# Strassen's weight sums in a feed-forward stage: which engine adds them, and the order of seven products

## The chip, the cores and the metric

The kernel runs on one core of one Trainium2 chip. The metric is the device time of one execution in microseconds (us), as the median of several runs. A profiled execution gives, beside its own time, the span from the first to the last instruction and a trace of every engine: PE (TensorE), whose weight loads are listed apart as PEld, DVE (VectorE), ACT (ScalarE), POOL (GpSimd) and SP (SyncE, which only issues transfers here).

## What is computed

One decoder layer on 512 tokens of width 1024, all in float32: a norm, two mixers (Mamba-2 and gated DeltaNet), a merge and projection, and then the feed-forward part, which alone is touched:

```python
FFN_HIDDEN = -(-8 * D_MODEL // (3 * 256)) * 256      # 2816
h = rmsnorm(x, norm_ffn_w[l])                        # 512 x 1024
gate, up = jnp.split(h @ w_ffn_in[l], [FFN_HIDDEN], axis=-1)   # w_ffn_in: 1024 x 5632
x = x + (jax.nn.silu(gate) * up) @ w_ffn_down[l]
...
return rmsnorm(x, final_norm_w)
```

## The kernel before

Every float32 matrix product is made of three matmuls. `split` (L265) parts a tile into a high half (`whi`, a cast on ACT) and a rest (`wlo`, a subtraction on DVE); `three` (L342) issues high x high, high x low and low x high into one PSUM bank. A weight block of 512 x 256 (512 KB) is a unit of the `stream`: it is loaded by SP (`fetch`, L303), split, and multiplied.

The hidden width 2816 is cut into 11 blocks of 256 columns (`fp`, 0 to 10). Block 0 is done in the plain way. Blocks 1 to 10 are done by Strassen's scheme in Winograd's form: the gate columns and the up columns of a block, each in an upper and a lower half of 512 rows, are four weight blocks b11, b12, b21 and b22, and seven products P1 to P7 of 512 x 256 weights with 512 x 256 activations take the place of eight. Their weights are b11 (P1), b21 (P2), t1 = b11 + b12 (P5), t3 = b12 + b22 (P7), b22 (P3), t2 = t1 + b22 (P6) and t4 = b21 + t2 (P4); signs are taken up by the sums of activations, which `h2_sums` makes once. A product is 24 matmuls of 256 columns (2 x 4 x 3).

Before the change (`ffn_units`, L1272) three tiles are loaded a block: x = b11, y = b22 and z = b21. The sums are made in them by transfers that POOL issues and that add to their destination (`gp.dma_start(..., accum_op=ALU.add)`). Once x has been split for P1, b12 is added to it (t1); once t1 has been split, b22 is added (t2); then z, after its own split, receives x (t4). y receives b12 after its split (t3). So each sum waits until the tile's earlier value has been read, and t4 also for t2 to land.

`ffn_block` (L1382) runs the products in the order `ORDER` into the PSUM banks that `BANK` names: A to F, one tile `pw` each. P1 and P2 share bank A: ACT copies P1 out of it to `p1`, and P2 is then added on top of it. `ffn_post` (L1298) forms the four output blocks from the banks: silu of the gate halves on ACT, sums u2, u3, c22 and the two multiplications (`act`) on DVE.

PE, DVE and ACT run their instructions in the order in which the program issues them; a planner (`Weave`, L34) with its own clock decides when which thread issues. SP's and POOL's order is set by a scheduler at build time. `ahead(2, 3)` (L278), called half-way through a product, splits up to two units ahead of it and has loads issued up to three units ahead of the splits; `Source.post` runs what follows a split (here the adding transfers). Buffers: 3 `whi`, 3 `wlo`, 3 `wst` (pool `wp`), 5 of `m4` (L209, where x and y lie), 8 PSUM banks.

After block 10, `down_job` (L1412) multiplies by w_ffn_down (tiles `pdn`).

Of the kernel before, what the change touches and what calls it, by code (L numbers as in the profile page):

```python
# [10 lines left out]
AF = mybir.ActivationFunctionType  # L11
ALU = mybir.AluOpType
ENG = mybir.EngineType

P = 128
T = 512
NT = T // P
D = 1024
# [15 lines left out]
class Weave:  # L34
# [65 lines left out]
    def finish(self, *events):  # L100
        for e in events:
            self.done[e] = self.cur

    def until(self, *events):

        def left():
            return [e for e in events
                    if e not in self.done or self.done[e] + SLACK > self.clock["PE"]]
        while left():
            assert self.threads or all(e in self.done for e in events), left()  # L110
            self.clock["PE"] += 100.0
            self.tick()
# [64 lines left out]
def hybrid_block_kernel(  # L177
# [8 lines left out]
    x = x[0]  # L186
# [12 lines left out]
    def nm(s):  # L199
        uid[0] += 1  # L200
        return f"{s}_{uid[0]}"

    def psum(s="p"):
        return ps.tile([P, 512], F32, tag="p", name=nm(s))

    def b8(shape, dtype=F32, s="b8"):
        return ap.tile([P] + list(shape), dtype, tag="b8", name=nm(s), bufs=NB8)

    def m4(shape, dtype=F32, s="m4"):  # L209
        return ap.tile([P] + list(shape), dtype, tag="m4", name=nm(s), bufs=NM4)  # L210

    def s2(shape, s="s2"):
        return ap.tile([P] + list(shape), F32, tag="s2", name=nm(s), bufs=NS2)

    wv = Weave(nc)
    te, ve, ac, gp, sy = wv.te, wv.ve, wv.ac, wv.gp, wv.sy
    start, spawn, until, finish, tick, side = wv.start, wv.spawn, wv.until, wv.finish, wv.tick, wv.side
# [60 lines left out]
    def ahead(n_split, n_load):  # L278

        main = wv.cur  # L280
        for i in range(len(splits), min(at[0] + n_split, len(stream))):
            _, a, b = stream[i]
            while len(loads) <= i:
                load()
            wv.cur = max(wv.clock["PE"], loads[i][1])
            src = stream[i][0]
            if getattr(src, "keep", False):
                both = b8([2, a, b], F32R, "wkeep")
                hi, lo = both[:, 0], both[:, 1]
            else:  # L290
                hi = wp.tile([P, a, b], F32R, tag="whi", name=nm("whi"))
                lo = wp.tile([P, a, b], F32R, tag="wlo", name=nm("wlo"))
            split(hi, lo, loads[i][0])
            if callable(src):
                src.post()
            splits.append((hi, lo, wv.cur))
            if len(loads) < min(i + 1 + n_load, len(stream)):
                load()
        while len(loads) < min(len(splits) + n_load, len(stream)):
            load()  # L300
        wv.cur = main

    def fetch(src, a, b, pool=None):  # L303
        if pool:
            st = pool([a, b], s="wst")
        else:
            st = wp.tile([P, a, b], F32, tag="wst", name=nm("wst"))
        sy.dma_start(st, src)
        return st
# [21 lines left out]
    def unit():  # L331
        ahead(1, 0)
        hi, lo, ready = splits[at[0]]
        at[0] += 1
        wv.clock["PE"] = max(wv.clock["PE"], ready)
        return hi, lo
# [537 lines left out]
    for b in range(2):  # L874
        z = Batch()
# [386 lines left out]
    ffn.a = {}  # L1262
    ffn.act = []
    NB = FH // 256
    ORDER = ("P1", "P3", "P2", "P5", "P7", "P6", "P4")
    BANK = {"P1": "A", "P3": "F", "P2": "A", "P5": "D", "P7": "C", "P6": "B", "P4": "E"}

    def ffn_src(r, c, fp):
        off = (FH if c else 0) + 256 * fp
        return w_ffn_in[512 * r:512 * r + 512, off:off + 256].rearrange("(k p) c -> p k c", p=P)  # L1270

    def ffn_units(fp):  # L1272
        if fp == 0:
            return [(Source(lambda r=r, c=c: fetch(ffn_src(r, c, 0), 4, 256), keep=True), 4, 256)
                    for c in range(2) for r in range(2)]
        w = Batch()

        def get(name, r, c, pool=None):
            setattr(w, name, fetch(ffn_src(r, c, fp), 4, 256, pool))
            return getattr(w, name)  # L1280

        def add(dst, src):
            gp.dma_start(dst, src, accum_op=ALU.add)

        def t2_t4():
            add(w.x, ffn_src(1, 1, fp))
            add(w.z, w.x)

        return [(Source(g, p), 4, 256) for g, p in (
            (lambda: get("x", 0, 0, m4), lambda: add(w.x, ffn_src(0, 1, fp))),  # L1290
            (lambda: get("y", 1, 1, m4), lambda: add(w.y, ffn_src(0, 1, fp))),
            (lambda: get("z", 1, 0), None),
            (lambda: w.x, t2_t4),
            (lambda: w.y, None),
            (lambda: w.x, None),
            (lambda: w.z, None))]

    def ffn_post(fp):  # L1298

        v = ffn.act[fp]  # L1300
        lo, hi = slice(0, 256), slice(256, 512)

        def half(s_):
            t = s2([512], s_)
            return t, t.rearrange("p (j t) -> p j t", j=2)

        bk = ffn.banks[fp]

        def two(t):
            return t.rearrange("p (j t) -> p j t", j=2)  # L1310

        if fp == 0:
            for name, s_ in (("c11", lo), ("c21", hi)):
                yield [("P", fp, name)]
                ac.activation(v[:, :, s_], two(bk[name]), AF.Silu)
                yield [("P", fp, name[:2] + "2")]
                ve.tensor_tensor(v[:, :, s_], two(bk[name[:2] + "2"]), v[:, :, s_], ALU.mult)
            finish(("ffn", fp))
            yield True
            return  # L1320
        yield [("P", fp, "P1")]
        p1, _ = half("p1")
        ac.copy(p1, bk["A"])
        finish(("p1", fp))
        yield [("P", fp, "P2")]
        ac.activation(v[:, :, lo], two(bk["A"]), AF.Silu)
        yield [("P", fp, "P6")]
        u2, _ = half("u2")
        u3, _ = half("u3")
        ve.tensor_tensor(u2, bk["B"], p1, ALU.add)  # L1330
        ve.tensor_tensor(u3, bk["C"], u2, ALU.add)
        ve.tensor_tensor(u2, bk["F"], u2, ALU.subtract)
        ve.tensor_tensor(u2, bk["D"], u2, ALU.add)
        ve.tensor_tensor(v[:, :, lo], two(u2), v[:, :, lo], ALU.mult)
        c22, c22v = half("c22")
        ve.tensor_tensor(c22, bk["D"], u3, ALU.subtract)
        yield [("P", fp, "P4")]
        ve.tensor_tensor(u3, bk["E"], u3, ALU.add)
        yield HOP
        ac.activation(v[:, :, hi], two(u3), AF.Silu)  # L1340
        yield HOP
        ve.tensor_tensor(v[:, :, hi], c22v, v[:, :, hi], ALU.mult)
        finish(("ffn", fp))
        yield True
# [3 lines left out]
    def ffn_start(fp):  # L1348
        ffn.banks[fp] = {}
        if fp % 2 == 0:  # L1350
            ffn.pair = b8([2, 2, T], F32, "act")
        ffn.act.append(ffn.pair[:, fp % 2])
        spawn(ffn_post(fp))

    def product(p, a, w, first, last, each=None):

        for j in range(2):
            cs = slice(j * P, (j + 1) * P)
            for kk in range(4):
                three(p[:, 256 * j:256 * j + 256], (w[0][:, kk, cs], w[1][:, kk, cs]), (a[0][:, kk], a[1][:, kk]),  # L1360
                      first and j == 0 and kk == 0, last and j == 1 and kk == 3, skip_group_check=True)
                if kk % 2:
                    tick()
            if j == 0 and each:
                each()
# [16 lines left out]
    def ffn_block(fp):  # L1382
        ffn_start(fp)
        bk = ffn.banks[fp]
        for name in ORDER:
            until(("a", name), *([("p1", fp)] if name == "P2" else []))
            fresh = BANK[name] not in bk
            if fresh:
                bk[BANK[name]] = psum("pw")
            w = unit()  # L1390
            product(bk[BANK[name]], ffn.a[name], w, fresh, True, lambda: ahead(2, 3))
            finish(("P", fp, name))

    for fp in range(NB):
        job(lambda fp=fp: ffn_block(fp) if fp else ffn_first(), *ffn_units(fp))
# [3 lines left out]
    def act_split():  # L1399

        for fp in range(NB):
            yield [("ffn", fp), ("P", NB - 1, ORDER[max(0, (fp + 1) // 2 - 1)])]
            w = b8([2, 2, T], F32R, "actw")
# [117 lines left out]
```

## Time and profile before

| | |
|---|---|
| median of three runs (1053.76 to 1055.57) | 1055.55 us |
| the profiled execution | 1055.14 us |
| its span, first to last instruction | 1053.4 us |
| PE busy of the span | 1008.9 us (96%) |
| DVE, ACT, POOL busy | 58%, 43%, 11% |
| products of blocks 1 to 10 | 680.9 to 926.7 us of the span |
| mean granted TensorE clock, of full speed | 0.99 |

The profiled execution lies 1.74 us above its span and 0.04% under the median. A matmul's end is modelled, so that PE counts as busy while a matmul drains; how much PE could still do is read from the distance between the starts of matmuls rather than from its busy share. A wait is put down to what came last.

### The profile page before, as it was taken

How to read it: one execution, taken by the hardware profiler on the slowest of the kernel's cores; microseconds unless marked ns; L12 is line 12 of the kernel's file. 1: busy time of each engine (PE TensorE's matmuls, PEld its weight loads, DVE VectorE, ACT ScalarE, POOL GpSimd, SP SyncE). 2: the span in 40 equal slices, each digit the busy share in tenths (PEclk: the TensorE clock that was granted, in tenths of full speed). 3: DMA queues.
4: the chain of work that ended last, by engine and by line, in shares of the span. 5: the costliest groups of instructions: out<-in, count | busy, mean ns of one | idle time of the engine just before them, and what ended most of it. 6: DMA issues, size and time to landing. Idle time of an engine off the chain costs nothing. (4 is left out here: it accounts for less than half of the span.)

```text
span 1053.4 us, 15628 instructions
## 1 busy us (share of the span) xinstructions
PE 1008.9 (96%) x6394; PEld 890.8 (85%) x6394; DVE 611.3 (58%) x904; ACT 453.9 (43%) x831; POOL 118.0 (11%) x144
## 2 busy tenths in 40 slices
PE   7999999999999999999999999989888888899997
PEld 5888878888888888788998899988888878888886
DVE  5665899545566867832255544755555555682422
ACT  5466445467857472022344223633333333452322
POOL 2041012100101210000010000111211211100000
PEclk9999999999999999999999999999999999999999
DMA  6242332121124533233322521657777776542222
GB/s 189 77 166 60 87 95 80 42 81 41 41 61 145 175 100 100 79 104 98 93 88 80 191 90 60 161 123 154 144 148 153 160 150 131 101 133 90 98 80 81
DMA packets 96072, 114.03 MB, mean 108 GB/s; under 512 B 6218, under 2 KB 86247, under 8 KB 95232
## 3 DMA queue, kind: packets, MB, share of 16 engines
q1 hardware_dynamic: 78718, 92.06, 28.3%
q0 software_dynamic: 17280, 20.97, 12.7%
q8 instruction: 50, 0.82, 0.3%
q14 instruction: 22, 0.18, 0.1%
q10 hardware_dynamic: 2, 0.00, 0.0%
HBM read 105.63 MB, written 2.15 MB: 102 GB/s over the span
## 5 line engine op out<-in xcount | busy, mean ns | idle before, releaser
L153 DVE TENSOR_TENSOR wlo<-wst,whi 128x1024 fp32r<-128x1024 f32 x184 | 225.7, 1236 | 297.1 <-ACT whi L153 290.9
L153 ACT CAST whi<-wst 128x1024 fp32r<-128x1024 f32 x184 | 190.9, 1048 | 285.5 <-PE pw L164 101.0
L164 PE MATMUL pw<-h2w,whi 128*128 128x256 f32 x1120 | 209.1, 288 | 11.2 <-ACT whi L153 11.2
L164 PE MATMUL pw<-hhi,whi 128*128 128x512 f32 (+1 forms) x496 | 196.4, 396 | 1.6 <-ACT whi L153 1.6
L164 PE MATMUL pw<-hhi,wlo 128*128 128x512 f32 (+1 forms) x496 | 191.2, 385 | 2.3 <-DVE wlo L153 2.3
L164 PE MATMUL pw<-hlo,whi 128*128 128x512 f32 (+1 forms) x496 | 190.6, 384 | 0.0
L164 PEld LDWEIGHTS pw<-h2w,whi 128*128 128x128 f32 x1120 | 177.4, 195 | 14.9 <-ACT whi L153 14.9
L164 PE MATMUL pw<-h2w,wlo 128*128 128x256 f32 x560 | 163.3, 292 | 16.7 <-DVE wlo L153 16.7
L164 PEld LDWEIGHTS pw<-h2w,wlo 128*128 128x128 f32 x560 | 109.2, 195 | 22.5 <-DVE wlo L153 22.2
L164 PEld LDWEIGHTS pw<-hhi,wlo 128*128 128x128 f32 x496 | 93.6, 189 | 21.9 <-DVE wlo L153 3.0
L164 PEld LDWEIGHTS pw<-hhi,whi 128*128 128x128 f32 x496 | 93.8, 189 | 18.1 <-ACT whi L153 1.8
L164 PE MATMUL pdn<-whi,actw 128*128 128x512 f32 x352 | 108.8, 390 | 0.0
L164 PEld LDWEIGHTS pw<-hlo,whi 128*128 128x128 f32 x496 | 93.8, 189 | 16.3
L164 PEld LDWEIGHTS pdn<-whi,actw 128*128 128x128 f32 x352 | 66.3, 188 | 13.9
L164 PE MATMUL pdn<-wlo,actw 128*128 128x512 f32 x176 | 68.6, 390 | 0.0
L153 POOL DMA_DIRECT2D wst<-in_w_ffn_in_dram x30 | 38.9, 1295 | 158.5 <-DVE wlo L153 154.7
L153 DVE SCALAR_TENSOR_TENSOR acc<-pw,pg,acc 128x511 f32<-128x511 f32 (+2 forms) x72 | 53.6, 747 | 2.8 <-ACT acc L153 0.9
L164 PE MATMUL pw<-yg,whi 128*128 128x512 f32 x128 | 42.9, 416 | 0.0
L164 PEld LDWEIGHTS pdn<-wlo,actw 128*128 128x128 f32 x176 | 33.2, 188 | 6.7
L164 PE MATMUL pt<-whi,hhi 128*128 128x256 f32 x128 | 36.5, 285 | 0.0
L164 PE MATMUL pt<-wlo,mgh 128*128 128x256 f32 x128 | 36.3, 284 | 0.1
L164 PE MATMUL pt<-whi,mgh 128*128 128x256 f32 x128 | 36.4, 284 | 0.0
(264 smaller groups left out, 1511.0 us busy)
## 6 DMA issues: line engine op xcount, KB each, us to landing
wst<-in_w_in_dram SPq DMA_DIRECT2D x68, 512.0 KB, 3.8
wst<-in_w_ffn_in_dram SPq DMA_DIRECT2D x34, 512.0 KB, 3.5
wst<-in_w_ffn_in_dram POOLq DMA_DIRECT2D x30, 512.0 KB, 5.9
wst<-in_w_ffn_down_dram SPq DMA_DIRECT2D x22, 512.0 KB, 3.7
decay<-gcd SPq DMA_DIRECT2D x6, 1024.0 KB, 4.7
wst<-wst POOLq DMA_DIRECT2D x10, 512.0 KB, 4.6
wst<-in_w_proj_gdn_dram SPq DMA_DIRECT2D x8, 512.0 KB, 3.4
wst<-in_w_proj_ssm_dram SPq DMA_DIRECT2D x8, 512.0 KB, 3.4
```

Source lines behind the costliest of these rows:

```text
L153: return f(out_, *args, **kw)
L164: return self.eng.matmul(out_, lhsT, rhs, **kw)
```

## The change

It replaces how the weight sums are made, the order of the seven products and the way the outputs are summed.

- Loads: five a block (b11, b21, b22, and a tile each for t1 and t3) in place of three. t1's tile is loaded with b11 and t3's with b22, right away, not after a split.
- Transfers that add: two a block in place of four. Each adds b12, to t1's tile and to t3's, as soon as that tile has landed.
- DVE: two new additions of 128 x 1024 a block (`sums`): t2 = t1 + b22 into a tile of its own, and t4 = t2 + b21 in place. They follow t1's split.
- The tiles t1, t2 and t3 lie in `m4`; b11, b21 and b22 in `wst`.
- Products: P1, P2, P5, P6, P7, P3, P4 in place of P1, P3, P2, P5, P7, P6, P4. P4 goes into P7's bank C, so that five banks a block are used in place of six; it waits for c22, which reads P7.
- Output sums: u2, w, c22, w and u2, five in place of six, and two multiplications as before.

```diff
-    ORDER = ("P1", "P3", "P2", "P5", "P7", "P6", "P4")
-    BANK = {"P1": "A", "P3": "F", "P2": "A", "P5": "D", "P7": "C", "P6": "B", "P4": "E"}
+    ORDER = ("P1", "P2", "P5", "P6", "P7", "P3", "P4")
+    BANK = {"P1": "A", "P2": "A", "P5": "D", "P6": "B", "P7": "C", "P3": "F", "P4": "C"}
...
-        def add(dst, src):
-            gp.dma_start(dst, src, accum_op=ALU.add)
-
-        def t2_t4():
-            add(w.x, ffn_src(1, 1, fp))
-            add(w.z, w.x)
+        def add(dst, r, c):
+            gp.dma_start(dst, ffn_src(r, c, fp), accum_op=ALU.add)
+
+        def t1():
+            get("t1", 0, 0, m4)
+            add(w.t1, 0, 1)
+            return w.t1
+
+        def t2():
+            get("b22", 1, 1)
+            w.t2 = m4([4, 256], s="t2")
+            return w.t2
+
+        def t3():
+            get("t3", 1, 1, m4)
+            add(w.t3, 0, 1)
+            return w.t3
+
+        def sums():
+            ve.tensor_tensor(w.t2, w.t1, w.b22, ALU.add)
+            ve.tensor_tensor(w.b21, w.t2, w.b21, ALU.add)
 
         return [(Source(g, p), 4, 256) for g, p in (
-            (lambda: get("x", 0, 0, m4), lambda: add(w.x, ffn_src(0, 1, fp))),
-            (lambda: get("y", 1, 1, m4), lambda: add(w.y, ffn_src(0, 1, fp))),
-            (lambda: get("z", 1, 0), None),
-            (lambda: w.x, t2_t4),
-            (lambda: w.y, None),
-            (lambda: w.x, None),
-            (lambda: w.z, None))]
+            (lambda: get("b11", 0, 0), None),
+            (lambda: get("b21", 1, 0), None),
+            (t1, sums),
+            (t2, None),
+            (t3, None),
+            (lambda: w.b22, None),
+            (lambda: w.b21, None))]
...
         u2, _ = half("u2")
-        u3, _ = half("u3")
+        w, wv_ = half("w")
         ve.tensor_tensor(u2, bk["B"], p1, ALU.add)
-        ve.tensor_tensor(u3, bk["C"], u2, ALU.add)
-        ve.tensor_tensor(u2, bk["F"], u2, ALU.subtract)
-        ve.tensor_tensor(u2, bk["D"], u2, ALU.add)
-        ve.tensor_tensor(v[:, :, lo], two(u2), v[:, :, lo], ALU.mult)
+        ve.tensor_tensor(w, bk["D"], u2, ALU.subtract)
+        yield [("P", fp, "P7")]
         c22, c22v = half("c22")
-        ve.tensor_tensor(c22, bk["D"], u3, ALU.subtract)
+        ve.tensor_tensor(c22, w, bk["C"], ALU.subtract)
+        finish(("c22", fp))
+        yield [("P", fp, "P3")]
+        ve.tensor_tensor(w, bk["F"], w, ALU.add)
+        ve.tensor_tensor(v[:, :, lo], wv_, v[:, :, lo], ALU.mult)
         yield [("P", fp, "P4")]
-        ve.tensor_tensor(u3, bk["E"], u3, ALU.add)
+        ve.tensor_tensor(u2, bk["C"], u2, ALU.add)
...
-            until(("a", name), *([("p1", fp)] if name == "P2" else []))
+            until(("a", name), *{"P2": [("p1", fp)], "P4": [("c22", fp)]}.get(name, []))
```

**First place: PE at the end of P1.** In these rows `h2w` is a split activation, and a `pw` tile a PSUM bank. PE before, from the last matmuls of P1 (bank pw_926) to the first of what follows:

```order
L164 MATMUL pw_926_6585<-h2w_838_5801,whi_918_6529 128x256 x2
L164 MATMUL pw_926_6585<-h2w_838_5801,wlo_919_6530 128x256
L164 MATMUL pw_929_6614<-h2w_869_6119,whi_924_6568 128x256 [waits Activation_49]
L164 MATMUL pw_929_6614<-h2w_869_6119,whi_924_6568 128x256
L164 MATMUL pw_929_6614<-h2w_869_6119,wlo_925_6569 128x256 [waits DVE_49]
```

What follows P1 is P3, in another bank (pw_929). PE after the change, at the same place of a later block (bank pw_963):

```order
L164 MATMUL pw_963_6827<-h2w_838_5801,whi_955_6774 128x256 x2
L164 MATMUL pw_963_6827<-h2w_838_5801,wlo_956_6775 128x256
L164 MATMUL pw_963_6827<-h2w_839_5816,whi_959_6807 128x256 [waits Activation_49]
L164 MATMUL pw_963_6827<-h2w_839_5816,whi_959_6807 128x256
L164 MATMUL pw_963_6827<-h2w_839_5816,wlo_960_6808 128x256 [waits DVE_49]
```

Now P2 follows, in the bank that P1 has just filled, with a wait for ACT.

**Second place: the transfers of a block.** POOL before, where wst_935 is x, wst_939 is y and wst_943 is z of one block, and the next row belongs to the next block:

```order
L153 DMA wst_935_6666<-in_w_ffn_in_dram 128x4x256 [waits DMAHW6_49,DVE_49]
L153 DMA wst_939_6698<-in_w_ffn_in_dram 128x4x256 [waits DMAHW0_49,DMASW5_49,DVE_49]
L153 DMA wst_935_6666<-in_w_ffn_in_dram 128x4x256 [waits DMASW4_49,DVE_49]
L153 DMA wst_943_6729<-wst_935_6666 128x1024 [waits DMAHW7_49,DMASW7_49,DMASW6_49]
L153 DMA wst_963_6894<-in_w_ffn_in_dram 128x4x256 [waits DMAHW1_49,DVE_49]
```

Each of the four stands behind a transfer or a split of the same block. POOL after, two rows a block, t1 and then t3 (wst_923 and wst_932 of block 3, wst_952 and wst_961 of block 4, wst_982 of block 5):

```order
L153 DMA wst_923_6514<-in_w_ffn_in_dram 128x4x256 [waits DMAHW1_49,DMAHW0_49,DVE_49]
L153 DMA wst_932_6581<-in_w_ffn_in_dram 128x4x256 [waits DMAHW1_49,DMASW1_49,DVE_49]
L153 DMA wst_952_6744<-in_w_ffn_in_dram 128x4x256 [waits DMAHW5_49,DMASW0_49,DVE_49]
L153 DMA wst_961_6811<-in_w_ffn_in_dram 128x4x256 [waits DMAHW6_49,DMASW3_49,DVE_49]
L153 DMA wst_982_6975<-in_w_ffn_in_dram 128x4x256 [waits DMAHW2_49,DMASW2_49,DVE_49]
```

What is left waits for the tile's own load and for an earlier user of its buffer. SP after, where wst_917 and wst_928 are b21 and b22 of block 3; wst_942, wst_952, wst_961, wst_946 and wst_957 are b11, t1, t3, b21 and b22 of block 4; and wst_972 is b11 of block 5:

```order
L153 DMA wst_917_6479<-in_w_ffn_in_dram 128x4x256 [waits DMAHW6_49,DMAHW2_49,DVE_49]
L153 DMA wst_928_6548<-in_w_ffn_in_dram 128x4x256 [waits DMAHW3_49,DVE_49]
L153 DMA wst_942_6678<-in_w_ffn_in_dram 128x4x256 [waits DMAHW7_49,DMAHW4_49,DVE_49]
L153 DMA wst_952_6744<-in_w_ffn_in_dram 128x4x256 [waits DMAHW5_49,DMASW0_49]
L153 DMA wst_961_6811<-in_w_ffn_in_dram 128x4x256 [waits DMASW3_49]
L153 DMA wst_946_6709<-in_w_ffn_in_dram 128x4x256 [waits DMAHW3_49,DVE_49]
L153 DMA wst_957_6778<-in_w_ffn_in_dram 128x4x256 [waits DMAHW0_49,DVE_49]
L153 DMA wst_972_6909<-in_w_ffn_in_dram 128x4x256 [waits DMAHW4_49,DMAHW1_49,DVE_49]
```

The loads of t1 and t3 of block 4 stand ahead of its b21, right behind its b11, which takes the buffer of block 3's b11.

**Third place: DVE through one block.** Before, from the split of t1 (wst_935, which is read again as t2 two rows on) to the split of the next block's b11 and the output sums:

```order
L153 TENSOR_TENSOR wlo_960_6861<-wst_935_6666,whi_959_6860 128x1024 [waits DMASW4_49,PE_49,Activation_49]
L153 TENSOR_TENSOR wlo_962_6891<-wst_939_6698,whi_961_6890 128x1024 [waits DVE_49,DMASW5_49,PE_49,Activation_49]
L153 TENSOR_TENSOR wlo_966_6923<-wst_935_6666,whi_965_6922 128x1024 [waits DVE_49,DMASW6_49,PE_49,Activation_49]
L153 TENSOR_TENSOR wlo_970_6954<-wst_943_6729,whi_969_6953 128x1024 [waits DMASW7_49,PE_49,Activation_49]
L153 TENSOR_TENSOR wlo_974_6985<-wst_963_6894,whi_973_6984 128x1024 [waits DMAHW1_49,PE_49,Activation_49]
L153 TENSOR_TENSOR u2_976_7008<-pw_972_6971,p1_958_6850 128x512 [waits PE_49]
L153 TENSOR_TENSOR u3_977_7009<-pw_968_6940,u2_976_7008 128x512 [waits DVE_49]
```

The splits of t1, t3, t2 and t4 each wait for an adding transfer (DMASW). After, from the split of t1 to c22:

```order
L153 TENSOR_TENSOR wlo_965_6844<-wst_952_6744,whi_964_6843 128x1024 [waits DMASW6_49,Activation_49]
L153 TENSOR_TENSOR t2_958_6780<-wst_952_6744,wst_957_6778 128x1024 [waits DMAHW0_49]
L153 TENSOR_TENSOR wst_946_6709<-t2_958_6780,wst_946_6709 128x1024 [waits DVE_49]
L153 TENSOR_TENSOR wlo_968_6876<-t2_958_6780,whi_967_6875 128x1024 [waits PE_49,Activation_49]
L153 TENSOR_TENSOR wlo_971_6906<-wst_961_6811,whi_970_6905 128x1024 [waits DMASW7_49,PE_49,Activation_49]
L153 TENSOR_TENSOR wlo_975_6937<-wst_957_6778,whi_974_6936 128x1024 [waits PE_49,Activation_49]
L153 TENSOR_TENSOR u2_978_6961<-pw_973_6923,p1_966_6861 128x512 [waits PE_49]
L153 TENSOR_TENSOR w_979_6962<-pw_969_6891,u2_978_6961 128x512 [waits DVE_49]
L153 TENSOR_TENSOR wlo_981_6972<-wst_946_6709,whi_980_6971 128x1024 [waits Activation_49]
L153 TENSOR_TENSOR c22_984_6997<-w_979_6962,pw_977_6954 128x512 [waits DVE_49,PE_49]
```

Two additions (t2, and t4 into wst_946) now stand between the split of t1 and that of t2, only the splits of t1 and t3 wait for an adding transfer, and the output sums stand apart from each other.

## Rows read from the trace of the kernel before

**Rows 1.** The page, busy us (share of the span) and instructions of each engine.

```profile
PE 1008.9 (96%) x6394; PEld 890.8 (85%) x6394; DVE 611.3 (58%) x904; ACT 453.9 (43%) x831; POOL 118.0 (11%) x144
```

**Rows 2.** Windows, the stage's stretch: us, busy us of engines, clock, DMA share, GB/s.

```profile
681.00:926.60 245.60, 217.64 (x1682) 208.28 (x1681) 138.29 (x151) 94.11 (x108) 44.97 (x38) 0.98 0.70 140
```

**Rows 3.** Instructions of tile pw on PE: duration ns min/median/max, first and last start.

```profile
L164 PE MATMUL pw<-h2w,whi x1120: 274/283/415, 680.9 to 926.1; 128*128 128x256 f32 x187
```

**Rows 4.** PE's waits in 681 to 927: us in total, times, longest us.

```profile
PE pw L164 <- DVE wlo L153: 16.7, 26, 0.8
PE pw L164 <- ACT whi L153: 11.2, 16, 2.0
```

**Rows 5.** Timeline of PE: start us, us, instruction, [idle before <-releaser].

```profile
767.88 0.40 PE L164 MATMUL pw<-h2w,whi 128*128 128x256 f32 x2
768.12 0.28 PE L164 MATMUL pw<-h2w,wlo 128*128 128x256 f32 x1
768.71 0.50 PE L164 MATMUL pw<-h2w,whi 128*128 128x256 f32 x2 [0.31 <-ACT whi L153]
769.97 0.39 PE L164 MATMUL pw<-h2w,wlo 128*128 128x256 f32 x1 [0.76 <-DVE wlo L153]
...
773.74 0.50 PE L164 MATMUL pw<-h2w,whi 128*128 128x256 f32 x2 [0.88 <-ACT whi L153]
```

**Rows 6.** Chain of waits, pieces of one block and its last: start us, us, what.

```profile
757.11 0.69 POOL wst L153
...
761.74 1.25 POOL wst L153
...
767.82 4.72 DMA wst<-wst
...
772.64 1.05 ACT whi L153
...
781.61 0.83 POOL wst L153
...
926.69 115.93 PE pdn L164 x510
```

**Rows 7.** DMA, 706 to 902: queue packets, MB, share; issues with KB, us to landing.

```profile
q0 software_dynamic: 13744, 16.70, 54.4%
q1 hardware_dynamic: 10713, 11.52, 18.4%
...
wst<-in_w_ffn_in_dram POOLq DMA_DIRECT2D x24, 512.0 KB, 5.9
wst<-in_w_ffn_in_dram SPq DMA_DIRECT2D x19, 512.0 KB, 3.7
```

**Rows 8.** Timeline of all engines around the end of a P1.

```profile
755.98 0.28 PE L164 MATMUL pw<-h2w,wlo 128*128 128x256 f32 x1
756.10 0.40 PE L164 MATMUL pw<-h2w,whi 128*128 128x256 f32 x2
756.30 0.59 ACT L153 COPY p<-pw 128x512 f32<-128x512 f32 x1 [1.95 <-PE pw L164]
```

**Rows 9.** Groups of instructions, 706 to 926: count, busy us, mean ns, idle before.

```profile
L153 DVE TENSOR_TENSOR wlo<-wst,whi 128x1024 fp32r<-128x1024 f32 x63 | 75.6, 1222 | 88.9 <-ACT whi L153 88.9
L153 ACT CAST whi<-wst 128x1024 fp32r<-128x1024 f32 x63 | 64.3, 1044 | 110.5 <-DMA wst<-in_w_ffn_in_dram 53.9 <-DMA wst<-wst 29.5 <-PE pw L164 27.1
...
L153 DVE TENSOR_TENSOR u<-pw,u 128x512 f32<-128x512 f32 x33 | 22.7, 689 | 0.8
```

**Rows 10.** Timeline of DVE, a sum of two float32 tiles in SBUF.

```profile
673.97 1.22 DVE L153 TENSOR_TENSOR hq<-hq,hq 128x1024 f32<-128x1024 f32 x1
```

**Rows 11.** Windows of 1 us behind waits of block 1; the clock is third from the end.

```profile
701.00:702.00 1.00, 0.45 (x3) 0.45 (x4) 1.00 (x2) 1.00 (x2) 0.00 (x0) 0.93 1.07 366
702.00:703.00 1.00, 1.00 (x7) 1.00 (x7) 1.00 (x2) 0.14 (x1) 0.07 (x1) 0.50 0.30 88
...
705.00:706.00 1.00, 1.00 (x9) 1.00 (x9) 0.97 (x2) 0.14 (x1) 0.00 (x0) 0.86 0.83 109
```

More of the change, by code (lines that the diff above doesn't have):

```diff
@@ L1328, in ffn_post @@
         u2, _ = half("u2")
-        u3, _ = half("u3")
+        w, wv_ = half("w")
         ve.tensor_tensor(u2, bk["B"], p1, ALU.add)
-        ve.tensor_tensor(u3, bk["C"], u2, ALU.add)
-        ve.tensor_tensor(u2, bk["F"], u2, ALU.subtract)
-        ve.tensor_tensor(u2, bk["D"], u2, ALU.add)
-        ve.tensor_tensor(v[:, :, lo], two(u2), v[:, :, lo], ALU.mult)
+        ve.tensor_tensor(w, bk["D"], u2, ALU.subtract)
+        yield [("P", fp, "P7")]
         c22, c22v = half("c22")
-        ve.tensor_tensor(c22, bk["D"], u3, ALU.subtract)
+        ve.tensor_tensor(c22, w, bk["C"], ALU.subtract)
[3 more added lines that the diff above has]
+        ve.tensor_tensor(v[:, :, lo], wv_, v[:, :, lo], ALU.mult)
         yield [("P", fp, "P4")]
-        ve.tensor_tensor(u3, bk["E"], u3, ALU.add)
+        ve.tensor_tensor(u2, bk["C"], u2, ALU.add)
         yield HOP
-        ac.activation(v[:, :, hi], two(u3), AF.Silu)
+        ac.activation(v[:, :, hi], two(u2), AF.Silu)
         yield HOP
```

## The prediction, made before the changed kernel was run

> **What bounds the kernel now.** The page's busy shares come first: PE at 96% [rows 1], so at first sight nothing that feeds PE is worth anything. But a matmul's end is modelled, so I looked next at the stage that the change touches and at how far apart its matmuls start. The stage runs from the first matmul of block 1 at 680.9 us [rows 3] to the first `pdn` matmul at 926.7 [rows 6]: 245.8 us. It holds 10 blocks x 7 products x 24 = 1680 matmuls. Where PE waits for nothing, two of them take 0.24 us from start to start (767.88 to 768.12) [rows 5], so 0.12 us each, and 1680 x 0.12 = 201.6 us. **So 44.2 us of this stage, 4.4 us a block, are not PE's work**, though its windows row shows PE busy for 217.6 of 245.6 us [rows 2].
>
> Does that close? PE's waits there come to 16.7 + 11.2 = 27.9 us in 42 waits [rows 4]. Each also hides 0.16 us (a modelled duration of 0.28 less the distance of 0.12) and restarts 0.10 us slower (a pair of 0.50 behind a wait, 0.40 elsewhere) [rows 5]: 42 x 0.26 = 10.9. The mean clock of 0.98 takes 2% of 245.6 us, 4.9 [rows 2]. Together 43.7 of the 44.2: the loss is waits, and what the clock does after them.
>
> Whom PE waits for names the splits, on ACT and DVE, but both are far from busy there (94 and 138 of 246 us [rows 2]). The chain of waits shows what stands behind them. One block of it [rows 6]: POOL issues a transfer that adds at 757.11, the next (into t2) at 761.74, the last (t2 into t4) at 767.82, when t2 has landed; t4 has landed by 772.64, when ACT casts it, and PE starts on it at 773.74 [rows 5]; behind that come DVE's subtractions and output sums, and with the following split POOL is back at 781.61: 24.5 us later, one block. This loop through POOL, the transfers, ACT and DVE is longer than PE's 7 x 24 x 0.12 = 20.2 us, and sets the pace.
>
> **The change, part by part.** *The loop goes.* t1 and t3 are now loaded and added to without a split before them. In SP's order the loads of t1 and t3 of block n+1 stand right behind that of its b11, which needs only that b11 of block n has been split; that split is done while block n-1 runs its last products. A load takes 3.7 us, an adding transfer 5.9 [rows 7]; even with both of the latter in a row, 3.7 + 2 x 5.9 = 15.5 us, issued some 18 us into block n-1, they land some 12 us into block n of 21, and are wanted when block n+1 starts. I cost them at nothing under that cover; what they cost without it is the slower rival below. t2 and t4 need no transfer.
>
> *The load on the DMA engines* stays short of full. In 196 us, 16.70 MB (32 transfers of 0.524 MB) that add took 54.4%, so 3.33 us of all engines each, and 11.52 MB (22) of plain loads 18.4%, 1.64 each [rows 7]. A block asked for 4 x 3.33 + 3 x 1.64 = 18.2 us; now 2 x 3.33 + 5 x 1.64 = 14.9, of a block of some 21 us: 70%, hidden. b21 of block n+1 waits until P3's b22 is split, about 12 us into block n, and is split itself from 18 on; b22 waits for t4's split, about 15 us in, and is wanted by `sums` at 25: at 3.7 us each both are in time, by 2 and 6 us.
>
> *DVE* gains two sums of 128 x 1024 at 1.22 [rows 10] and loses one of 128 x 512 at 0.69 [rows 9]: 7 x 1.22 + 2 x 1.22 + 7 x 0.69 = 15.8 us a block in place of 14.1. That is 75% of 21 us, not a bound by its sum. Its order could still hurt: both sums stand ahead of t2's split. With P1 starting at 0, u2 runs to 0.9, silu on ACT to 1.6, the multiplication to 2.3, the split of t1 (cast 1.04 [rows 9] on ACT, then 1.22) to 3.9, the sums to 6.3, t2's split to 7.5; P6 starts at 9.6. About 2 us remain. Later splits and sums find their inputs some 2 to 3 us before they are due, and c22 has read bank C two us before P4 writes it. So hidden, zero.
>
> *P2 behind P1 in one bank* is the one wait that the change adds on PE's path. P2's first matmul may not touch the bank before ACT has copied it. P1's last matmul starts at 755.98 and ends at 756.26; ACT's copy starts at 756.30 and takes 0.59, to 756.89 [rows 8]; an ACT result lets PE go 0.05 later (a cast from 772.64 [rows 6] for 1.05, PE at 773.74 [rows 5]): 756.94. PE went on at 756.10 [rows 8], since P3 in another bank came next. So 0.84 us, and 0.10 for the restart: **0.94 us a block, 9.4 us in ten**. Nothing else on PE can fill it; queued behind are all the block's products. ACT is free when the copy is due, as the silu and the cast ahead of it end near 2.7 us and P1 at 2.9. In block 10 one cast of the activations (1.04) stands there too; I add 0.4, between 0 and 1.0. Below zero this term can't go: the bank is the same.
>
> *Block 1 and the stage's borders.* The activations of P6 and P7 are made in the old order, in time for their new places. t1 of block 1 is loaded and added to much earlier, behind loads of other stages, where before two loads of this stage stood: zero. P4 in P7's bank, one bank fewer: zero.
>
> *Sum.* 201.6 + 9.4 + 0.4 = 211.4 us in place of 245.8: 34.4 us less. The profiled execution was 1055.14 us, so **1020.7 us**; it stands 0.04% under the median of 1055.55, and I make nothing of that difference.
>
> **The rivals.**
>
> *A. The clock falls in every block.* Behind block 1's waits at 700 the granted clock is 0.93, then 0.50 for three us (703 and 704 read as 702), then 0.86 [rows 11]: half speed, 1.2 GHz, and 0.07 + 1.5 + 0.14 = 1.7 us lost. If the gap behind each P1 brought that, ten blocks lose 17 us: 1037.7. Against it: the stage's 4.9 us are about three such falls in ten blocks, though a block had four waits on average [rows 4], of 0.3 to 0.9 us and close together [rows 5]; one gap a block of 0.84 is less. The Trainium skill (TensorE: Matmul & The Clock Gate, section "A second HAM failure mode: psum-queue depth-cycling") speaks for A: short idles between groups of matmuls, with PSUM banks in rotation, make the clock go up and down. By that rule, the result is A's 1037.7; the trace so far bears it out in the minority of blocks. 8%.
>
> *B. DVE's queue comes late.* The sums leave about 2 us ahead of P6. If the load of b22 or a stretched instruction uses that up, each block loses another 0.5 to 1.5 us: 1025.7 to 1035.7. For it: DVE at 75%, strictly in order, and its output sums now wait for single products in between. Against it: every slack above is over 1 us. 18%.
>
> *C. Transfers still set the pace.* At 70% load a transfer may take longer than its median; if b21 or t1 is late in many blocks, half of the gain is lost: 1055.14 - 17.2 = 1037.9. 4%.
>
> *D. No cost behind P1.* If the copy were over before P2 is due, PE runs at 0.12 us throughout: 1055.14 - 44.2 = 1010.9. Rows 8 speak against it. 4%.
>
> *E. Slower: t1 lands late, and holds P2 up.* On ACT the cast of t1 stands ahead of the copy of P1, so that a late t1 delays the very next product. Say its load is held back by one block more than I read from SP's order, because its buffer or b11's comes free late: issued 18 us into block n, it lands at 21.7, the addition at 27.6, the cast ends at 28.7, the copy at 29.3; P2 was due at 21.1 + 2.9 = 24.0. Then a block takes 20.16 + 5.3 + 0.1 = 25.6 us in place of 24.6, so 1055.1 + 10 = 1065. It decides from 4.4 us of wait a block. The order after the change speaks against it: block 4's t1 stands ahead of block 4's b21. 3%.
>
> **How the numbers follow.** My forecast has 63%, A 8, B 18, C 4, D 4, E 3. The likeliest is the forecast, 1020.7. Its own bounds are 1019 (the cost behind P1 at its bare 0.84, nothing in block 10) to 1024 (some 0.3 us a block left). To hold 8 in 10 the range goes from 1016 to 1036, which takes in B (63 + 18 = 81%) and a few us below the bound for what the clock gives back at the stage's end. Faster by over 0.2%, which is about what a measurement of this kernel can tell from no change, are all cases but E and a small part of C: 0.96; within 0.2% 0.01; slower 0.03.
>
> **What would show it.** In the profile after: the stage from the first matmul of block 1 to the first `pdn` takes 211 us; PE's waits there are about ten of 0.8 us, released by ACT's copy to `p` (right), where casts and subtractions released them before; DVE's share of the stage rises from 56% to about 75%, the DMA share stays near 0.70, the clock is 1.00. Wrong: PE waits for `whi` or `wlo` in most blocks (B, C), ACT waits for an adding transfer before the cast of t1 (E), a clock of 0.5 behind each P1 (A), or waits at P2 that are missing (D).

## The result, and the profile after

The changed kernel takes **1020.58 us** in the median of four runs (1019.94 to 1021.14), the kernel before beside it 1055.56 (1053.76 to 1056.59): a ratio of 0.967, with a 95% interval of 0.9653 to 0.9687. 35.0 us are gone. The profiled execution took 1021.12 us, its span is 1019.4.

First the page after, busy us (share of the span) and instructions of each engine, as [rows 1]:

```profile
PE 996.5 (98%) x6394; PEld 885.7 (87%) x6394; DVE 630.2 (62%) x914; ACT 455.3 (45%) x831; POOL 96.1 (9%) x124
```

By busy shares hardly anything has happened: PE from 96% to 98%. The stage tells more. Its matmuls, then PE's waits in 676 to 900 (total us, times, longest), then the stretch as a windows row (us, busy us of PE, PEld, DVE, ACT, POOL, clock, DMA share, GB/s):

```profile
L164 PE MATMUL pw<-h2w,whi x1120: 280/283/387, 681.4 to 892.3; 128*128 128x256 f32 x187
```

```profile
PE pw L164 <- ACT p L153: 7.0, 10, 0.9
```

```profile
681.00:892.00 211.00, 203.99 (x1681) 201.96 (x1680) 160.39 (x165) 96.31 (x109) 21.83 (x17) 1.00 0.67 163
```

Against [rows 3, 4, 2]: the first matmul of the stage starts at nearly the same time (681.4, before 680.9), the last 33.8 us sooner (892.3, before 926.1). Of 42 waits for casts and subtractions none is left; ten are there that were not, one a block, all for ACT's copy `p`. DVE went from 56% to 76% of the stretch, the DMA share from 0.70 to 0.67, the clock from 0.98 to 1.00.

The chain of waits says whom the stage now waits for. The end of one block and the next, and the last block (start us, us, what):

```profile
706.19 20.43 PE pw L164 x168
726.62 0.02 issue
726.64 0.59 ACT p L153
727.24 0.04 issue
...
853.83 17.56 PE pw L164 x144
...
873.71 0.94 ACT actw L153
874.65 0.49 ACT p L153
...
875.19 17.53 PE pw L164 x144
892.72 3.43 PE pdn L164 x15
```

POOL and the transfers, which stood in each block of the chain before [rows 6], are not in it: it is PE for 20.43 us, the copy, PE again. P2 of the one block starts at 706.19, that of the next at 727.24 + 0.04 = 727.28: a block takes 21.09 us in place of 24.5. In block 10 the cast of the activations (`actw`, 0.94) stands ahead of the copy, and P2 starts at 875.19, 21.36 us after block 9's (853.83).

The hand-over in PE's timeline (start us, us, instruction, [idle before <-releaser]), P1's last matmul and P2's first pair:

```profile
705.23 0.28 PE L164 MATMUL pw<-h2w,wlo 128*128 128x256 f32 x1
706.19 0.50 PE L164 MATMUL pw<-h2w,whi 128*128 128x256 f32 x2 [0.68 <-ACT p L153]
```

Start to start that is 0.96 us where 0.12 is usual, so 0.84 lost, and the pair takes 0.50 where 0.40 is usual.

And DVE in the same place of the next block, whose P1 ends at 726.6:

```profile
726.10 1.23 DVE L153 TENSOR_TENSOR wlo<-wst,whi 128x1024 fp32r<-128x1024 f32 x1 [0.25 <-ACT whi L153]
727.24 1.22 DVE L153 TENSOR_TENSOR t<-wst,wst 128x1024 f32<-128x1024 f32 x1
728.49 1.23 DVE L153 TENSOR_TENSOR wst<-t,wst 128x1024 f32<-128x1024 f32 x1
729.63 1.22 DVE L153 TENSOR_TENSOR wlo<-t,whi 128x1024 fp32r<-128x1024 f32 x1
```

The split of t1, the two new sums, the split of t2, without a gap. t2's rest is there at 730.85. P6 is due two products after P2's start, at 727.28 + 0.10 + 2 x 24 x 0.12 = 733.1: 2.3 us of slack.

Last the DMA from 706 to 892 (queue: packets, MB, share; issues with KB and median us to landing), as [rows 7]:

```profile
q1 hardware_dynamic: 20552, 21.61, 36.8%
q0 software_dynamic: 8448, 8.39, 29.9%
...
wst<-in_w_ffn_in_dram POOLq DMA_DIRECT2D x16, 512.0 KB, 7.0
```

Two adding transfers a block in place of four. Each takes longer to land than before, 7.0 us in place of 5.9, and nobody waits for it.

### The profile page after: what moved, and what is told of

The parts are those of the page before. It is cut to its first block, busy times and chain, and to the rows that moved or that the text cites. A ratio compares the mean times of both kernels' runs of the same rounds, so it can differ in the third digit from the quotient of the medians.

```text
span 1019.4 us, 15625 instructions
## 1 busy us (share of the span) xinstructions
PE 996.5 (98%) x6394; PEld 885.7 (87%) x6394; DVE 630.2 (62%) x914; ACT 455.3 (45%) x831; POOL 96.1 (9%) x124
## 5 line engine op out<-in xcount | busy, mean ns | idle before, releaser
L153 DVE TENSOR_TENSOR wlo<-wst,whi 128x1024 fp32r<-128x1024 f32 x174 | 215.0, 1236 | 224.7 <-ACT whi L153 218.5
L153 ACT CAST whi<-wst 128x1024 fp32r<-128x1024 f32 x174 | 182.1, 1048 | 231.4 <-PE pw L164 125.8
L164 PE MATMUL pw<-h2w,whi 128*128 128x256 f32 x1120 | 203.0, 284 | 7.0 <-ACT p L153 7.0
L164 PEld LDWEIGHTS pw<-h2w,whi 128*128 128x128 f32 x1120 | 174.6, 192 | 9.0 <-ACT p L153 9.0
L164 PE MATMUL pw<-h2w,wlo 128*128 128x256 f32 x560 | 158.4, 283 | 0.0
L153 POOL DMA_DIRECT2D wst<-in_w_ffn_in_dram x20 | 25.9, 1296 | 243.0 <-DMA wst<-in_w_ffn_in_dram 143.3
```

The lines of the kernel that those rows point to most:

```text
L153: return f(out_, *args, **kw)
L164: return self.eng.matmul(out_, lhsT, rhs, **kw)
```

## Experiments

Two questions. Which part of the change brought the gain, and what does each term of the sum weigh by itself? My theory: the gain is that t1, t3, t2 and t4 left the loop through POOL, and the only thing paid for it on PE's path is the copy of P1. The rivals: that the other order and the other output sums bring part of it; that DVE or the transfers are near to being the bound, so that the result holds by luck. The first four kernels ran beside a kernel before of 1055.86 us, the last four beside one of 1053.74; small differences between the two sets are read from the ratios and the stages, not from the times.

### The new sums with the old order: e4_old_order

The loads, adding transfers and DVE sums are those of the change; the order, the six banks and the output sums are those of before.

```diff
-    ORDER = ("P1", "P2", "P5", "P6", "P7", "P3", "P4")
+    ORDER = ("P1", "P3", "P2", "P5", "P7", "P6", "P4")
...
-            (lambda: get("b21", 1, 0), None),
+            (lambda: get("b22", 1, 1), None),
+            (lambda: get("b21", 1, 0), None),
             (t1, sums),
-            (t2, None),
             (t3, None),
-            (lambda: w.b22, None),
+            (t2, None),
             (lambda: w.b21, None))]
```

> The weight sums of the changed kernel alone, with the products in the old order (P1, P3, P2, P5, P7, P6, P4), in six banks and with the old output sums. Theory (the loop through the adding transfers was the whole loss; order and output sums add only the wait behind P1): faster than the changed kernel, 1011 to 1016 us, the upper end if the old clump of six output operations on DVE still makes PE wait some 0.4 us at P3. Rival (the new order and the output sums carry part of the gain): 1025 us or more.

Measured: 1010.86 us (1009.52 to 1011.26), 0.9576 of the kernel before (0.956 to 0.9592). In its trace PE waits for nothing from 676 to 900. The windows row of its stage:

```profile
679.00:880.70 201.70, 201.64 (x1681) 201.44 (x1680) 162.60 (x172) 95.02 (x108) 21.83 (x17) 1.00 0.69 171
```

201.7 us for 1680 matmuls are 0.12 each, the distance without a wait. **So the whole gain, and more, is that of the weight sums.** The rest of the change takes 10 us back: the old order puts P3, in a bank of its own, between P1 and P2, and the copy of P1 runs behind it. This version beats both kernels. (Part of its lead over the changed kernel in the profiled executions, some 2 us, lies ahead of the stage: in the ten traces of this study the stage starts between 679.0 and 681.9 us, and I have not followed up why.)

### P2 in its own bank: e1_own_bank

The order of the change, but P2 goes to bank E and starts afresh there; P1 is left out of the gate half.

```diff
-    BANK = {"P1": "A", "P2": "A", ...
+    BANK = {"P1": "A", "P2": "E", ...
...
-        ac.activation(v[:, :, lo], two(bk["A"]), AF.Silu)
+        ac.activation(v[:, :, lo], two(bk["E"]), AF.Silu)
```

> The changed kernel with P2 in a bank of its own (E) in place of P1's bank A, so that PE need not wait for ACT's copy; P1 is left out of the gate half of the output. Theory (the wait behind P1 costs 0.94 us a block and nothing hides behind it): 9.4 + 0.4 us less, 1011 us, no waits of PE on ACT's copy left. Rival (PE's waits would show up elsewhere, at the next split or output sum, once this one is gone): 1016 to 1021, new waits on whi or wlo.

Measured: 1011.3 us (1010.0 to 1012.1), ratio 0.9577 (0.9563 to 0.9592), and no wait of PE in the stage (681.6 to 883.0 us). Taking the shared bank away alone gives 9.3 us, where the prediction had put 9.4 + 0.4 on it. The new order and output sums cost nothing else: on PE's path e1 and e4 are equal.

### P5 between P1 and P2: e3_p5_between

The same cure with the computation whole. The sums move behind b21's split.

```diff
-    ORDER = ("P1", "P2", "P5", "P6", "P7", "P3", "P4")
+    ORDER = ("P1", "P5", "P2", "P6", "P7", "P3", "P4")
...
-            (lambda: get("b21", 1, 0), None),
-            (t1, sums),
+            (t1, None),
+            (lambda: get("b21", 1, 0), sums),
```

> The changed kernel with the products in the order P1, P5, P2, P6, P7, P3, P4: t1 is split before b21, and the sums follow b21's split. Theory: the copy of P1 runs behind P5, so the 0.94 us a block are gone and PE starts a matmul every 0.12 us: 1011 us. Rival (the sums now stand one unit nearer to t2's split, about 2.9 us later for the same due time, so that DVE's slack of 2.4 us ahead of P6 is used up): waits on wlo at P6 of about 0.5 us a block, 1016 us or more.

Measured: 1012.85 us (1011.32 to 1015.7), ratio 0.9596 (0.9577 to 0.9615). One wait is left in the stage, 1.9 us in the last block (until 882.69) for the cast of the activations; the ten for the copy are gone. Behind that one wait the clock fell (it is third from the end):

```profile
884.00:885.00 1.00, 1.00 (x6) 1.00 (x6) 0.96 (x3) 0.00 (x0) 0.00 (x0) 0.50 0.81 301
```

### The copy twice: e2_copy_twice

```diff
         ac.copy(p1, bk["A"])
+        ac.copy(p1, bk["A"])
```

> The changed kernel with ACT's copy of P1 issued twice. Theory (the copy lies bare on PE's path in every block): 0.5 to 0.6 us a block more, 1026 us. Rival (something else lets P2 go later than the copy): below 1022.

Measured: 1026.91 us (1026.48 to 1028.01), ratio 0.9728 (0.9713 to 0.9742), so 6.3 us more than the changed kernel. Its chain of waits through one block:

```profile
769.98 0.59 ACT p L153
...
770.60 0.59 ACT p L153
...
771.24 20.42 PE pw L164 x168
```

Each microsecond that ACT puts between P1 and P2 is a microsecond of the kernel, ten times over; nothing takes it up. PE now idles 1.3 to 1.6 us in each block, and the clock still stays at 1.00.

### Only t2 and t4 back on transfers: e5_t2_by_dma

t1 and t3 as in the change. t2 and t4 are made as before, by adding transfers in t1's and b21's tiles.

```diff
-            ve.tensor_tensor(w.t2, w.t1, w.b22, ALU.add)
-            ve.tensor_tensor(w.b21, w.t2, w.b21, ALU.add)
+            add(w.t1, 1, 1)
+            gp.dma_start(w.b21, w.t1, accum_op=ALU.add)
```

> The changed kernel with t2 and t4 made by adding transfers again (b22 onto t1's tile once it has been split, then t1's tile onto b21), t1 and t3 as in the change. Theory (the sums' way round by transfers is longer than the time to P6): t1 is split 3.9 us into a block, the transfer lands some 6.5 us later, cast and subtraction end at 12.8, P6 is due at 9.6: about 3 us a block more, 1050 us, PE waits on whi and wlo of t2. Rival (loading t1 and t3 early is what brought the gain, and the sums on DVE are only tidier): 1021 us.

Measured: 1059.94 us (1058.70 to 1061.46), ratio 1.0061 (1.0036 to 1.0086): the gain is gone and a little more. PE's waits in the stage, and one block in its chain:

```profile
PE pw L164 <- ACT whi L153: 21.2, 10, 7.4
PE pw L164 <- ACT p L153: 7.0, 10, 0.9
PE pw L164 <- DVE wlo L153: 7.0, 10, 0.8
```

```profile
774.92 10.00 PE pw L164 x70
...
785.96 1.28 POOL wst L153
787.25 4.41 issue
...
791.67 5.91 DMA wst<-in_w_ffn_in_dram
...
798.73 1.24 DVE wlo L153
...
800.01 8.66 PE pw L164 x70
...
823.70 8.66 PE pw L164 x70
```

The 4.41 us that the chain calls issue are POOL's wait for t1's split, as the timeline of DVE and POOL shows ([idle before <-releaser]):

```profile
790.15 1.23 DVE L153 TENSOR_TENSOR wlo<-wst,whi 128x1024 fp32r<-128x1024 f32 x1 [0.24 <-ACT whi L153]
791.67 1.28 POOL L153 DMA_DIRECT2D wst<-in_w_ffn_in_dram  x1 [4.42 <-DVE wlo L153]
```

A loop through POOL and the transfers is back: P4, its output sum `u` and silu, t1's cast and split, t2's addition, t2's cast and split, P6. POOL's issue at 785.96 is another addition. t1's split ends at 790.15 + 1.23 = 791.38, t2's addition is issued at 791.67 and lands 5.91 us later, at 797.58: 6.2 us after the split, where I had taken 6.5. From one P6 to the next it is 800.01 - 774.92 = 25.1 us where the clock stood at 0.50 from 775 to 778, and 823.70 - 800.01 = 23.7 in the next block, 2.6 more than 21.09, where I had put about 3. So the price of the way round was about right. What the expectation left out is block 1 and the clock. In block 1 PE waits 7.4 us: POOL issues t2's addition right behind another one, at 687.46, and that one waited for its tile's load, until 686.90. The clock stood at 0.50 behind that wait until 702, and behind two later ones (748 to 754, 775 to 778). The stage takes 679.9 to 931.53, 251.6 us: 201.6 of matmuls, 35.7 of waits, 31 x 0.26 that a wait hides and costs at its restart, and 6 that are left for the clock.

### Only t1 back in b11's tile: e6_t1_in_place

t2 and t4 on DVE as in the change, but t1 is made where b11 lies, after its split.

```diff
         def t1():
-            get("t1", 0, 0, m4)
-            add(w.t1, 0, 1)
             return w.t1
...
-            (lambda: get("b11", 0, 0), None),
+            (lambda: get("t1", 0, 0, m4), lambda: add(w.t1, 0, 1)),
```

> The changed kernel with t1 made in b11's tile after b11's split, as before the change; t2 and t4 on DVE. Theory (t1 lands late and the cast of t1 stands ahead of the copy of P1 on ACT, so that P2 waits): split of b11 at 17.8 us into the block before, landed at 24 to 25, cast and copy to 26.7, P2 was due at 24.0: about 2 us a block more than the changed kernel, 1036 to 1042 us; waits of PE on ACT's copy of 2 to 3 us. Rival (one link alone doesn't bind): 1021 us.

Measured: 1057.67 us (1049.97 to 1059.06), ratio 1.0023 (1.0 to 1.0046). Again all of the gain is gone, though one sum of four was moved. It isn't the load on the DMA engines: their share of the stage is 0.51 here, and was 0.70 in the kernel before. PE's waits, and one block in the chain:

```profile
PE pw L164 <- ACT p L153: 30.5, 10, 4.4
```

```profile
771.08 1.24 DVE wlo L153
...
772.61 7.78 DMA wst<-in_w_ffn_in_dram
...
780.48 1.04 ACT whi L153
781.53 0.50 ACT p L153
...
782.07 13.14 PE pw L164 x95
```

This is the prediction's rival E at work: a late t1, its cast on ACT ahead of the copy of P1, and P2 behind both; PE names the copy, and the cause is the transfer. The transfer takes 7.78 us, and 8.23 in the next block; three plain loads are issued in the 3 us before it, from 769.82 on. The waits come to some 3 us a block, the upper end of what I had expected; the rest is the clock. Windows of 1 us behind that wait (the clock is third from the end):

```profile
782.00:783.00 1.00, 0.94 (x4) 0.94 (x5) 1.00 (x2) 0.01 (x1) 0.00 (x0) 0.51 1.22 196
783.00:784.00 1.00, 1.00 (x7) 1.00 (x6) 0.97 (x2) 0.00 (x0) 0.00 (x0) 0.50 0.50 77
...
786.00:787.00 1.00, 1.00 (x11) 1.00 (x10) 0.31 (x1) 0.30 (x1) 0.00 (x0) 1.00 0.00 0
```

PE starts again at 782.07 at half speed, 1.2 GHz, and is back at 1.00 by 786: 7 matmuls in a microsecond in place of 11. The stage takes 680.1 to 930.07, 250.0 us: 201.6 of matmuls, 30.5 of waits, 10 x 0.26 that a wait hides and costs at its restart, and 15.3 that are left for the clock: behind eight of the ten waits it stood at 0.50 for 3 to 7 us.

### Two and three sums more on DVE: e7_more_dve2, e8_more_dve3

The sum for t2 is issued three times and four times, to weigh the slack ahead of P6.

```diff
             ve.tensor_tensor(w.t2, w.t1, w.b22, ALU.add)
+            ve.tensor_tensor(w.t2, w.t1, w.b22, ALU.add)
+            ve.tensor_tensor(w.t2, w.t1, w.b22, ALU.add)
```

> The changed kernel with the sum t2 issued three times in a row on DVE, two operations of 1.2 us more a block. Theory (2.4 us of slack ahead of P6 in the trace of the changed kernel): 2.3 us more, just hidden: 1020 to 1023 us. Rival (DVE's queue sets the pace): 23 us more, 1044.

> The same with three operations more a block, 3.4 us. Theory: the slack of 2.4 us is overdrawn by about 1 us, PE waits on wlo at P6: 10 us more, 1029 to 1034. Rival (DVE's queue sets the pace already): 34 us more, 1055; rival (there is more slack than read): 1021.

Measured, in two runs each: 1025.07 us, ratio 0.9731 (0.9703 to 0.9759), with two more; 1038.54, ratio 0.9859 (0.983 to 0.9888), with three. From the first matmul of block 1 to the last of block 10 these are 215.9 us (680.4 to 896.3) and 230.1 (680.1 to 910.2), where the changed kernel has 210.9: 2.5 us of DVE's time in each block cost 5.0 in all, 3.7 cost 19.2. With three the chain of waits has another loop in it:

```profile
840.23 0.70 DVE u L153
...
841.49 1.05 ACT whi L153
...
842.56 1.23 DVE wlo L153
843.78 1.15 DVE t L153
...
844.96 1.24 DVE t L153
...
848.79 1.06 ACT whi L153
...
849.88 1.23 DVE wlo L153
...
851.15 1.94 PE pw L164 x14
```

The last output sum `u` waits for P4; its silu and t1's cast follow on ACT, then t1's split and the sums on DVE, t2's cast and t2's split, and P6 waits for that. From `u` to P6 10.92 us pass here, and the next `u` follows when P6 to P4 have run: 22.50 us from one `u` to the next (862.73). A sum less shortens the loop by 1.24: with none added it would be 18.8, with two 21.26. PE's own period with the copy is 21.09. The three periods in the traces, 21.09, 21.25 (748.85 - 727.60 in the chain of e7) and 22.50, are the larger of the two each time; 18.8 was worked out from the 22.50, so that the test of it is e7, 21.25 for 21.26. So the slack is 21.09 - 18.8 = 2.3 us, as the timeline of the changed kernel had it, and three extra sums overrun it by 1.4 us a block, 14 us. My expectation for e8 stopped about there; the other 5 us are the first and the last block: a wait of 2.1 us in block 1 and one of 1.9 in block 10, where casts of the activations stand too, and behind each of them the clock at 0.50 for some 3 us. Of e7's 5.0 us the loop, at 21.25 - 21.09 = 0.16 a block, is some 1.5; the rest are waits in blocks 1 and 10 (0.9, 0.8 and 1.3 us) that the changed kernel doesn't have.

## Why the prediction was right

Predicted 1020.7 us, measured 1020.58. That the median agrees to 0.1 us is luck, as the four runs spread over 1.2 us; the stage, 211.4 said and 211.3 measured, is the fairer test. Since a total can be right by errors that cancel, step by step:

- **The loop through POOL, the transfers, ACT and DVE sets the pace, and goes.** It went: no piece of POOL or of a transfer in the chain of the stage. e4 ties the gain to the weight sums alone. e5 and e6 add what the prediction didn't say: there were two chained parts, t1 behind b11's split and t2 and t4 behind t1's, and either of them, left chained beside the rest of the change, brings the old time back (with the wait for the copy of P1 in it). One link of the loop was misread: [rows 6] has POOL go from its issue at 757.11 to the one into t2 at 761.74, with 3.90 us of issue between them. POOL's timeline of the kernel before shows what it waited for there:

```profile
761.71 1.28 POOL L153 DMA_DIRECT2D wst<-in_w_ffn_in_dram  x1 [3.32 <-DVE wlo L153]
```

That is t1's split (760.19 to 761.42), which stands behind an output sum, its silu and t1's cast, as in the loops of e5 and e8. The loop's period, 24.5 us, and the forecast are the same either way.

- **PE's floor of 201.6 us**, from the distance of matmul starts and not from the busy share: e4's stage is 201.7.
- **P2 behind P1, 0.94 us a block.** Period 21.09 less 168 x 0.12 = 20.16 is 0.93; e1 without it is faster by 9.3 us. The reading by which [rows 8] priced an event that they don't show (last matmul's end, ACT's copy, PE's restart) held in each part.
- **The last block, 0.4 extra, between 0 and 1.0.** The stage runs from 681.4 to 892.7, 211.3 us. Ten hand-overs of 0.93 account for 9.3 of the 9.7 us over 201.6, and 0.4 is left. Of it 0.27 is block 10's (21.36 less 21.09); the rest lies at the stage's borders, which the prediction had at zero. So the term was of the right size, in part by luck.
- **DVE hidden.** Its share is 76% (said: 75%), t2's split ends at 730.85, 7.3 us after the block's start at 723.6, which is the start of P1's last matmul, 726.33, less 23 x 0.12 (said: 7.5), the slack is 2.3 us (said: about 2). e7 and e8 show where it ends. Rival B was real as a mechanism, with its threshold beyond what this change asks for.
- **Transfers hidden.** Share 0.67 (said: 70%). The landing of an adding transfer was under-priced, 7.0 in place of 5.9; the cover of a whole block took that up. Rival C didn't come about.
- **The clock, rival A.** Each of the 1-us windows from 681 to 892 shows 1.00. One gap of 0.7 us (changed kernel), and even of 1.3 to 1.6 (e2), in each 21 to 22 us left it there. The length of a gap alone doesn't decide: in the kernel before, the clock fell behind waits that were no longer than those of e2, but close together (PE's timeline, then a windows row):

```profile
798.65 0.50 PE L164 MATMUL pw<-h2w,whi 128*128 128x256 f32 x2 [0.71 <-ACT whi L153]
799.91 0.39 PE L164 MATMUL pw<-h2w,wlo 128*128 128x256 f32 x1 [0.76 <-DVE wlo L153]
...
802.00:803.00 1.00, 1.00 (x7) 1.00 (x7) 0.97 (x2) 0.00 (x0) 0.58 (x1) 0.50 0.86 295
```

The Trainium skill (TensorE: Matmul & The Clock Gate, section "A second HAM failure mode: psum-queue depth-cycling") warns that short idles between groups of matmuls, if frequent enough, make the clock go up and down. The three falls in the kernel before (from 701, 800 and 923 on) agree with that in kind; one gap a block, in the changed kernel and in e2, brought none.

- **Rival D's figure**, 1010.9, is what e4 (1010.86) and e1 (1011.3) reach, e1 by a bank of its own for P2, e4 by P3 between P1 and P2 in the shared bank; the prediction had it right that the change itself wouldn't.
- **Rival E** does exist, as e6 shows: 1057.67 where the prediction had 1065. It needs t1's load or addition to hang on the split, which the change had just undone.

What went wrong were sizes in the experiments, each on the same side: e5 to e8 came out slower than expected. I priced waits without the clock that falls behind some of them (e5, e6, e8) and without the first and the last block (e5, e7, e8); in e6 t1 also landed 8.1 us after b11's split (772.32 to 780.38), where I had put 6 to 7.

## What to carry to other kernels

When a matmul group is to add to a bank that another engine must read first, put a product in another bank between them: here that is worth 10 us of 1020, and the kernel before had it. Sums of weights belong off the chain from split to product, either as transfers that hang on nothing of the block, or on an engine whose queue has the room; if one of several chained parts stays, the gain may be nothing. Where the chain names a long piece issue, look at that engine's timeline: twice here it was POOL's wait for a split on DVE. To price an added wait that the trace doesn't show, build it from the hand-overs that the trace does show, and find the slack of the engine that takes the work by the period of its loop, not by its busy share: DVE at 76% had room for 2.3 us a block and no more.

## What was not expected of the hardware

- How long a transfer that adds takes to land varies much: in the median 5.9 us in the kernel before and 7.0 in the changed kernel, 5.6 to 5.9 for t2's in four blocks of e5's chain, and 6.6 to 8.2 for t1's in e6. I put that down to what else is under way at the time, which no run here isolates. On the DMA engines of the changed kernel each takes 29.9% of 186 us for 16 of them, 3.5 us, a plain one 36.8% for 41, 1.7.
- The price of a wait on PE isn't proportional, and its length alone doesn't tell it. Ten waits of 0.7 us, or of 1.3, left the clock at 1.00. In e6 eight of nine waits of 2.3 to 4.4 us were followed by 3 to 7 us at half speed, 15 us in all beside 30.5 of waiting; the ninth, of 3.0 us, was not. Shorter ones were too: a single one of 1.9 us in e3, and two of 0.7 to 0.8 close together in the kernel before. What decides it is open.
